# The softmax rows of a two-layer decoder trunk are scaled on Pool, head by head, instead of on VectorE and ScalarE

## The chip, the core and the metric

The kernel runs on one core of a Trainium2 chip. The metric is device microseconds (us) of one execution. The kernel before takes 322.24 us, the median of 3 runs (322.04 to 323.86). Five engines work side by side, each through its own queue in a fixed order: TensorE (PE, with its weight loads as PEld), VectorE (DVE), ScalarE (ACT), GpSimd (POOL, "Pool" in the text) and SyncE (SP), which here issues the loads of the weights. They meet at semaphores.

## The reference, cut to what matters

Two layers; x is 256 tokens by 1024 features, float32. In each layer

```
mod = silu(c) @ W_ada + b_ada -> (shift, scale, gate)
h   = RMSNorm(x) * (1 + scale) + shift
[q_A k_A v_A g_A | q_B k_B v_B g_B] = h @ W_in          (1024 x 4096)
A: 8 heads of 64, mixture of three causal dilated window attentions
B: 8 heads of 64, block-sparse attention (256 tokens are one block, so plain causal)
y   = RMSNorm([o_A*silu(g_A) | o_B*silu(g_B)] @ W_out);  x <- x + gate * y
```

q and k carry a partial rotary turn. For both branches the kernel computes softmax(scores + mask) @ v for each head: with 256 tokens the mixture of branch A is one softmax whose mask holds the logarithm of how many of the three patterns see a key. The change concerns one step of that softmax: the division of each row of exponentials by its sum.

## The kernel before, in words

Weights arrive by DMA as "pieces" of 128 x 1024 float32 (tile raw, 6 buffers). To keep float32 accuracy on PE, each is split in two: ACT copies the leading bits to whi (L205), DVE subtracts whi from raw and gets wlo (L212, 128 x 512 each). PE then makes three products for each k-tile, hi x whi, lo x whi and hi x wlo (L513; L526 for the gate chunks). A raw buffer comes free, and SP issues the next load, once DVE has made wlo of it. Other pieces are rows of W_ada; DVE "folds" those into running sums (L364, tiles acc_g and acc_ss).

PE's order is written out by hand as a list of slots (one slot is half a chunk of the input projection for 128 tokens), and the attention of two heads (a "pair") is threaded between slots: st_T (transposes of q and k), st_S one slot later (scores), st_X two slots after st_S (transposes of the softmax rows, L625), st_V one or two slots later (times v). There are 16 pairs: 4 of branch A and 4 of B in each layer. The text numbers them 1 to 16 in the order of the program; 1 to 8 are layer 0. The other engines' orders are made by a scheduler from the program; each engine then works through its queue strictly in that order.

The softmax step in st_S, for the two heads i of a pair, in tile z (128 x 384: queries 0-127 with keys 0-127, and queries 128-255 with all 256 keys):

- L601, DVE: scores plus mask into z, with the row minimum; L604, ACT: exponential, with the row sum into den.
- L608, DVE: one reciprocal of the four sums of the pair, rc.
- L614 and L612: the four blocks of z times rc. Three go to DVE (128, 256 and 128 columns), and one, the second head's 256 columns, to ACT (the table NACT picks it).

Then PE transposes z (L625). qkl (L579) is a DVE subtraction for the next pair's scores that reads the PSUM tile "t"; L625 needs a buffer of that tile, so it can wait for L579 too.

Pool has little to do: constants and two small inputs at the start, zeroing acc_g once a layer (L352), and the one-column arithmetic of the norms (L462 to L465).

Of the kernel before, what the change touches and what calls it, by code (L numbers as in the profile page):

```python
# [9 lines left out]
F32 = mybir.dt.float32  # L10
F32R = mybir.dt.float32r
I32 = mybir.dt.int32
AF = mybir.ActivationFunctionType
# [3 lines left out]
P = 128  # L17
# [5 lines left out]
# Slots: one product of half a chunk each, counted in a layer up to 32. Pairs of values: one for each layer.  # L23
# Where the heads of a branch start, and the distance of scores, transposes and outputs from there
AT_A, AT_B = ((12, 10), (22, 22))
# where branch A is gated; where the gate and the second token tile's h are made
# [4 lines left out]
# buffers for weights as loaded and for their two parts  # L31
NRAW, NHI, NLO = (6, 9, 8)
FOLD = 2048
# how far the splitting of weights runs ahead; what goes to the scalar engine; where W_ada's parts are due
AHEAD = (-12, 4)
H_AT = (2, 2)
NACT = (3,)
XACT = (0, 1)
ADA0, ADA1, ADA2 = ((2, 1), (6, 1), (23, 2))
# The start. GROUPS: k-tiles whose modulation is made together. FIRST_LOADS: a, b W_ada of a group, f a k-tile of  # L40
# W_in for the first two chunks, s, v quarters of chunks 2 and 5. FIRST_STEPS: T small inputs, R rotary tables, K masks,
# n, x norm and transposes of x, a, b, m modulation of a group, h, l its h in two parts, f, g a weight piece in two
# parts, p its products, w, y and s, v the same for chunks 2 and 5, k products that keep the array busy.
# [7 lines left out]
# theta ** (-2 i / RD) in float32  # L51
# [5 lines left out]
def turn_constants():  # L57
    """For units 2^20, 2^8, 2^-4: frac(unit / 2 pi) cut into parts of 12 bits, over the unit."""
    from fractions import Fraction
    pi = Fraction("3.14159265358979323846264338327950288419716939937510582097494459230781640628620899")  # L60
    rows = []
    for e in (20, 8, -4):
        u = Fraction(2) ** e
        f = u / (2 * pi)
        f -= f.numerator // f.denominator
        f1 = Fraction((f * 4096).numerator // (f * 4096).denominator, 4096)
        g = f - f1
        f2 = Fraction((g * 2 ** 24).numerator // (g * 2 ** 24).denominator, 2 ** 24)
        f3 = g - f2
        rows.append([float(f1 / u), float(f2 / u), float(f3 / u)])  # L70
    return rows
# [3 lines left out]
def trunk(ctx: ExitStack, tc: tile.TileContext, x, c, positions, pre_gain, post_gain,  # L75
# [19 lines left out]
    # ---------------------------------------------------------------- small inputs  # L95
    # rows: positions, c, the gains of the first norm, the shift and scale parts of b_ada
# [15 lines left out]
    # ---------------------------------------------------------------- weight stream  # L112
# [6 lines left out]
    def load_weights(src, key, r0, c0):  # L119
        """Two k-tiles of 512 columns"""  # L120
        nc.sync.dma_start(piece(key), src[r0:r0 + 2 * P, c0:c0 + CW].rearrange("(k p) n -> p k n", p=P))

    def load_first(key):
        """A k-tile for the first two chunks"""
# [3 lines left out]
    def load_group(key):  # L128
        """W_ada's columns for the shift and scale of a group of features: some of the rows"""
# [8 lines left out]
    def load_ada(key):  # L138
        """i < KT: a k-tile, the shift or the scale of all features; else the gate, a k-tile"""
# [25 lines left out]
    # Order of the weight stream: with each layer's products, what the next modulation needs.  # L165
    # a, b: W_ada for a group of features; f: the rows of W_in that it scales; s, v: quarters of other chunks
# [10 lines left out]
    # what the modulation needs, after the halves named  # L177
# [20 lines left out]
    def split_piece(key, a, b, low=True):  # L198
        """Parts a to b of a piece: hi holds the first 12 bits of each weight, lo the other 12."""
# [19 lines left out]
    # ---------------------------------------------------------------- constants  # L219
# [7 lines left out]
    # the table set of Silu serves until the first Exp  # L227
# [4 lines left out]
    # masks, to be added to minus the scores: [queries 0-127 x keys 0-127 | queries 128-255 x keys 0-255]  # L232
# [31 lines left out]
    # silu(c) and the gains of the first norm by feature on partitions  # L264
# [19 lines left out]
    def make_rope():  # L284
        # rotary tables: the angle in turns, reduced exactly, for any position
# [48 lines left out]
    # ---------------------------------------------------------------- modulation  # L334
# [31 lines left out]
    def mod_of(l, part, nb=4):  # L366
        """Rows 0, 32, .. of part in columns: [feature in its block, block, row]."""
# [11 lines left out]
    def ada_sum(l):  # L379
        """Sums over partitions of acc; 512 features to each group of 32 columns of the array."""  # L380
# [67 lines left out]
    def gate_end(l, h):  # L448
        """Sums over partitions of acc, on every partition, times the gain of the second norm."""
# [7 lines left out]
    # ---------------------------------------------------------------- norms  # L457
    def rstd_of(ms, other=None):
        """(sum of means + EPS) ** -0.5"""
# [10 lines left out]
    def parts_of(l, g):  # L470
        """hi and lo of half the features of h (or of a branch's output), for all tokens"""
# [32 lines left out]
    # ---------------------------------------------------------------- products with weights  # L504
    def product(bank, act, t, key, first, last, part=None):
        """The four k-tiles of a half, or two of them."""
# [9 lines left out]
    def gate_product(bank, act, u, key, hf):  # L516
        """Features 256 u to 256 (u + 1) of a chunk on partitions, all tokens: the weights stay, h streams."""
# [12 lines left out]
    # ---------------------------------------------------------------- attention  # L530
# [36 lines left out]
    def st_T(br, p):  # L567
# [5 lines left out]
        # the first 128 queries and keys; for the others, queries and all keys in two parts  # L573
# [10 lines left out]
    def st_S(br, p):  # L584
# [11 lines left out]
        den = ap.tile([P, 2, NT, 2], F32, name="den", bufs=4)  # L596
        pp = []
        for i in range(2):
            z = ap.tile([P, NS], F32, name="z", bufs=4)
            for t, (a, b) in enumerate(SC):  # L600
                nc.vector.tensor_tensor_reduce(z[:, a:b], bank[i][:, a:b], masks[br][:, a:b], 1.0, 3.0e38,  # L601
                                               ALU.add, ALU.min, accum_out=den[:, 0, t, i:i + 1])
            for t, (a, b) in enumerate(SC):
                nc.scalar.activation(z[:, a:b], z[:, a:b], AF.Exp, bias=den[:, 0, t, i:i + 1], scale=-1.0,  # L604
                                     accum_out=den[:, 1, t, i:i + 1])
            pp.append(z)
        rc = ap.tile([P, NT, 2], F32, name="rc", bufs=2)
        nc.vector.reciprocal(rc, den[:, 1])  # L608
        for i in range(2):
            for t, (a, b) in enumerate(SC):  # L610
                if 2 * t + i in NACT:
                    nc.scalar.activation(pp[i][:, a:b], pp[i][:, a:b], AF.Copy, scale=rc[:, t, i:i + 1])  # L612
                else:
                    nc.vector.tensor_scalar_mul(pp[i][:, a:b], pp[i][:, a:b], rc[:, t, i:i + 1])  # L614
# [19 lines left out]
    def st_V(br, p):  # L634
        """Outputs of two heads: [feature, token]"""
# [19 lines left out]
    def finish(br, p, src=None):  # L655
        """Outputs of two heads times the gate, in two parts"""
# [38 lines left out]
    # ---------------------------------------------------------------- the program  # L695
# [46 lines left out]
    def first_product(q, j, ci):  # L742
        """k-tile 2 q + j with chunk ci, both token tiles"""
# [14 lines left out]
    def early(t, part):  # L758
        """The first half of chunk 5, kept in the memory until the second one is due."""
# [33 lines left out]
    def keep_clock(n):  # L793
        """Products that nothing reads: the array's clock stays down until it has been busy for a while."""
# [134 lines left out]
```

## Time and profile before

| what | value |
|---|---|
| median of 3 runs | 322.24 us (322.04 to 323.86) |
| span of the profiled execution, the only time the profile gives of it | 321.5 us |
| PE, DVE, ACT, Pool busy | 299.6, 245.6, 203.5, 12.3 us |
| Pool instructions | 46 |
| mean granted TensorE clock | 0.996 of full speed |

The span is 0.7 us under the median of the runs. An engine's busy time counts the rows of its instructions; rows of neighbours overlap by a little on PE, DVE and ACT, so that three DVE products of 0.28, 0.35 and 0.28 us show as one merged entry of 0.74 us. In an answer on waits, the engine named first sat idle and the one behind the arrow ended it.

### The profile page before, as it was taken

Reading aid. Unit: us, or ns where it says so; the run is one execution under the profiler, and the core shown is the slowest. Engines: PE = TensorE matmul, PEld = TensorE weight load, DVE = VectorE, ACT = ScalarE, POOL = GpSimd, SP = SyncE. Lnnn points to the kernel's source line nnn. Section 1 sums busy time; section 2 is a strip of 40 time slices with the busy share of each in tenths; the row PEclk is TensorE's granted clock in tenths of the full one; section 3 lists DMA queues with packets and bytes.
Section 4 is the critical chain, followed back from the end, with each engine's and each line's share of the span. In section 5 each row is a group of like instructions: output and inputs, shape, how many; then the busy total and the mean of one; then the engine's idle time right before and its main releaser. Section 6 shows DMA issues by size and latency. Waiting matters only on the chain.

```text
span 321.5 us, 5293 instructions
## 1 busy us (share of the span) xinstructions
PE 299.6 (93%) x1817; PEld 237.6 (74%) x1817; DVE 245.6 (76%) x637; ACT 203.5 (63%) x435; POOL 12.3 (4%) x46
## 2 busy tenths in 40 slices
PE   0898899989999999999999899999999999999992
PEld 0565475867777789877687688877777799997881
DVE  4866773998998989898879899789785566786122
ACT  3646161959777469879568457578675579984100
POOL 3100001000000000000020300000000000000001
PEclk9999999999999999999999999999999999999998
DMA  8999988899798787586858549997765433000011
GB/s 253 342 351 302 346 262 308 293 348 317 247 302 265 259 287 202 173 280 233 285 185 282 178 129 303 350 320 231 228 215 177 132 132 131 2 1 2 0 65 65
DMA packets 37394, 70.63 MB, mean 220 GB/s; under 512 B 2492, under 2 KB 12790, under 8 KB 37368
## 3 DMA queue, kind: packets, MB, share of 16 engines
q1 hardware_dynamic: 36960, 69.22, 65.7%
q10 hardware_dynamic: 408, 1.09, 0.9%
q8 instruction: 14, 0.23, 0.3%
q14 instruction: 12, 0.10, 0.1%
HBM read 69.24 MB, written 1.05 MB: 219 GB/s over the span
## 4 chain that ended last, share of the span: by engine, by line
PE 57%; DMA 14%; DVE 13%; ACT 10%; issue 2%; SPq 1%; POOL 1%; ACTq 0%; DVEq 0%; POOLq 0%
PE mm L513 31%; PE mm L526 7%; DMA raw<-in_w_in_dram 5%; DVE wlo L212 4%; DMA raw<-in_w_ada_dram 4%; ACT whi L205 4%; DMA raw<-in_w_out_dram 3%; PE mm L753 3%; ACT z L604 3%; PE o L642 3%; PE o L414 2%; PE t L625 2%; DVE acc_ss L364 2%; DMA rows<-in_b_ada_dram 1%; PE t L513 1%
## 5 line engine op out<-in xcount | busy, mean ns | idle before, releaser
L212 DVE TENSOR_TENSOR wlo<-raw,whi 128x512 fp32r<-128x512 f32 x160 | 102.4, 685 | 8.0 <-PE mm L513 3.1
L205 ACT ACTIVATE whi<-raw 128x1024 fp32r<-128x1024 f32 (+1 forms) x88 | 84.4, 979 | 37.2 <-DMA raw<-in_w_in_dram 19.8
L513 PE MATMUL mm<-whi,hi 128*128 128x512 f32 x200 | 81.7, 408 | 0.0
L513 PE MATMUL mm<-wlo,hi 128*128 128x512 f32 x200 | 79.1, 395 | 0.0
L513 PE MATMUL mm<-whi,lo 128*128 128x512 f32 x200 | 79.0, 395 | 0.0
L513 PEld LDWEIGHTS mm<-whi,hi 128*128 128x128 f32 x200 | 37.6, 188 | 10.5 <-issue 1.7
L513 PEld LDWEIGHTS mm<-wlo,hi 128*128 128x128 f32 x200 | 37.6, 188 | 8.8
L513 PEld LDWEIGHTS mm<-whi,lo 128*128 128x128 f32 x200 | 37.7, 189 | 8.1 <-DVE lo L502 0.5
L526 PE MATMUL mm<-hi,whi 128*128 128x256 f32 x128 | 37.2, 291 | 0.0
L526 PE MATMUL mm<-hi,wlo 128*128 128x256 f32 x128 | 36.1, 282 | 0.0
L526 PE MATMUL mm<-lo,whi 128*128 128x256 f32 x128 | 36.0, 281 | 0.0
L604 ACT ACTIVATE z<-z,den 128x128 f32<-128x128 f32 x64 | 28.3, 445 | 3.8 <-DVE den L601 3.8
L526 PEld LDWEIGHTS mm<-hi,whi 128*128 128x128 f32 x128 | 24.1, 188 | 1.2 <-issue 0.2
L526 PEld LDWEIGHTS mm<-lo,whi 128*128 128x128 f32 x128 | 24.2, 189 | 0.2
L526 PEld LDWEIGHTS mm<-hi,wlo 128*128 128x128 f32 x128 | 24.1, 188 | 0.0
L364 DVE SCALAR_TENSOR_TENSOR acc_g<-raw,cs,acc_g 128x1024 f32<-128x1024 f32 x16 | 20.5, 1281 | 4.1 <-DMA raw<-in_w_ada_dram 4.1
L687 DVE TENSOR_TENSOR tmp<-mm,gate 128x512 f32<-128x512 f32 x8 | 5.5, 688 | 16.8 <-ACT sq L685 16.8
L364 DVE SCALAR_TENSOR_TENSOR acc_ss<-raw,cs,acc_ss 128x1024 f32<-128x1024 f32 x14 | 17.5, 1276 | 0.0
L685 ACT ACTIVATE sq<-mm 128x512 f32<-128x512 f32 x8 | 4.7, 593 | 19.8 <-PE mm L513 19.8
L625 PE MATMUL t<-ident,z 128*128 128x128 f32 x96 | 15.0, 282 | 2.4 <-DVE qkl L579 1.1
L625 PEld LDWEIGHTS t<-ident,z 128*128 128x128 f32 x96 | 10.6, 140 | 6.2 <-issue 1.7
L628 ACT ACTIVATE pT<-t 128x384 f32<-128x384 f32 x32 | 14.0, 491 | 1.2 <-PE t L625 1.2
(173 smaller groups left out, 454.9 us busy)
## 6 DMA issues: line engine op xcount, KB each, us to landing
raw<-in_w_in_dram SPq DMA_DIRECT2D x64, 512.0 KB, 5.2
raw<-in_w_ada_dram SPq DMA_DIRECT2D x32, 512.0 KB, 4.7
raw<-in_w_ada_dram SPq DMA_DIRECT2D x32, 256.0 KB, 5.0
raw<-in_w_out_dram SPq DMA_DIRECT2D x16, 512.0 KB, 5.1
xs<-in_x_dram SPq DMA_DIRECT2D x2, 512.0 KB, 4.3
gate<-in_post_norm_gain_dram ACTq DMA_DIRECT2D x2, 512.0 KB, 4.9
out_dram<-xs SPq DMA_DIRECT2D x4, 256.0 KB, 2.1
rows<-in_b_ada_dram ACTq DMA_DIRECT2D x2, 8.0 KB, 4.9
```

The costliest lines, as they stand in the source:

```text
L205: nc.scalar.activation(hi_q[key][:, a:b, :], raw[:, a:b, :], AF.Copy)
L212: nc.vector.tensor_sub(lo[:, d, :], raw[:, d, :], hi[:, d, :].bitcast(F32))
L364: nc.vector.scalar_tensor_tensor(a[:, sl], r[:, sl], cs[:, k:k + 1], a[:, sl], op0=ALU.mult, op1=ALU.add)
L414: nc.tensor.matmul(pm[32 * j:32 * j + 32, :w], csz[:, k, :], r[:, i * w:(i + 1) * w], start=k < 4, stop=k >= 4, tile_position=(0, 32 * j))
L513: nc.tensor.matmul(bank, a[:, k, t, :], w[:, k % 2, :], start=first and k + i == 0, stop=last and k == KH - 1 and i == 2)
L526: nc.tensor.matmul(bank[:, b * S:(b + 1) * S], w[:, k % 2, c0:c0 + P], a[:, k].rearrange("p t q -> p (t q)"), start=hf + b + k + i == 0, s ...
L604: nc.scalar.activation(z[:, a:b], z[:, a:b], AF.Exp, bias=den[:, 0, t, i:i + 1], scale=-1.0, accum_out=den[:, 1, t, i:i + 1])
L625: nc.tensor.transpose(pt[:, b * P:(b + 1) * P], pp[i][:, b * P:(b + 1) * P], ident)
L628: nc.scalar.activation(d, pt[:, :NS], AF.Copy)
L642: nc.tensor.matmul(ob[i * HD:(i + 1) * HD, q0:q0 + P], v[:, t, h], res[i][:, c0:c0 + P], start=t == 0, stop=n != 1, tile_position=(0, i * HD))
L687: nc.vector.tensor_mul(yg[:, sl], yb.pop((t, cc)), gate[l][:, sl])
L753: nc.tensor.matmul(mm[0, ci, t], a[:, k, t, :], w[:, ci, :], start=q == 0 and j == 0 and i == 0, stop=q == 3 and j == 1 and i == 2)
```

## The change

The reciprocal is taken for each head (of two sums, not four) as soon as that head's exponentials are there, and all four blocks of z are multiplied on Pool, two after each reciprocal. The products on DVE (L614) and on ACT (L612) and the table NACT are gone. The comments are also taken out, so that line numbers in the changed kernel are 1 to 3 lower (L608 is the reciprocal in both; the product on Pool is L610, wlo is L211, the fold L363, qkl L578).

```
-NACT = (3,)
...
-        den = ap.tile([P, 2, NT, 2], F32, name="den", bufs=4)
+        dens = ap.tile([P, 2, 2, NT], F32, name="den", bufs=4)
+        rcs = ap.tile([P, 2, NT], F32, name="rc", bufs=2)
         pp = []
         for i in range(2):
+            den, rc = dens[:, i], rcs[:, i]
             z = ap.tile([P, NS], F32, name="z", bufs=4)
...
-                                               ALU.add, ALU.min, accum_out=den[:, 0, t, i:i + 1])
+                                               ALU.add, ALU.min, accum_out=den[:, 0, t:t + 1])
...
-                nc.scalar.activation(z[:, a:b], z[:, a:b], AF.Exp, bias=den[:, 0, t, i:i + 1], scale=-1.0,
-                                     accum_out=den[:, 1, t, i:i + 1])
+                nc.scalar.activation(z[:, a:b], z[:, a:b], AF.Exp, bias=den[:, 0, t:t + 1], scale=-1.0,
+                                     accum_out=den[:, 1, t:t + 1])
+            nc.vector.reciprocal(rc, den[:, 1])
+            for t, (a, b) in enumerate(SC):
+                nc.gpsimd.tensor_scalar_mul(z[:, a:b], z[:, a:b], rc[:, t:t + 1])
             pp.append(z)
-        rc = ap.tile([P, NT, 2], F32, name="rc", bufs=2)
-        nc.vector.reciprocal(rc, den[:, 1])
-        for i in range(2):
-            for t, (a, b) in enumerate(SC):
-                if 2 * t + i in NACT:
-                    nc.scalar.activation(pp[i][:, a:b], pp[i][:, a:b], AF.Copy, scale=rc[:, t, i:i + 1])
-                else:
-                    nc.vector.tensor_scalar_mul(pp[i][:, a:b], pp[i][:, a:b], rc[:, t, i:i + 1])
         pr[br, p] = pp
```

The orders of PE and SP are the same in both kernels. What the scheduler makes of DVE's queue shows at two places. The first is pair 7 (layer 0, branch B, third pair), DVE from the last subtraction before the reciprocal on. Before:

```order
L364 SCALAR_TENSOR_TENSOR acc_ss<-raw,cs,acc_ss 128x1024 x2
L608 RECIPROCAL rc<-den 128x4
L212 TENSOR_TENSOR wlo<-raw,whi 128x512
L614 TENSOR_SCALAR z<-z,rc 128x128
L614 TENSOR_SCALAR z<-z,rc 128x256
L614 TENSOR_SCALAR z<-z,rc 128x128
L579 TENSOR_TENSOR qkl<-t,qkh 128x384
```

and with the change:

```order
L211 TENSOR_TENSOR wlo<-raw,whi 128x512 x3
L608 RECIPROCAL rc<-den 128x2
L363 SCALAR_TENSOR_TENSOR acc_ss<-raw,cs,acc_ss 128x1024
L608 RECIPROCAL rc<-den 128x2
L578 TENSOR_TENSOR qkl<-t,qkh 128x384
L363 SCALAR_TENSOR_TENSOR acc_ss<-raw,cs,acc_ss 128x1024
L211 TENSOR_TENSOR wlo<-raw,whi 128x512 x3
```

A fold now stands between the two heads' reciprocals. The same stands in pairs 1, 3 and 8; in pairs 2, 4, 5 and 6 it is one wlo subtraction.

The second place is layer 1, DVE in pair 10 (branch A, second pair), with the change:

```order
L363 SCALAR_TENSOR_TENSOR acc_g<-raw,cs,acc_g 128x1024
L608 RECIPROCAL rc<-den 128x2 x2
L546 TENSOR_TENSOR ra<-qk,cose 128x128
L547 TENSOR_TENSOR rb<-qk,sine 128x8x8
L548 TENSOR_TENSOR rb<-qk,sine 128x8x8
L549 TENSOR_TENSOR qk<-ra,rb 128x8x16
L578 TENSOR_TENSOR qkl<-t,qkh 128x384
L211 TENSOR_TENSOR wlo<-raw,whi 128x512 x4
```

Here, and in five more of the eight pairs of layer 1, both reciprocals stand together, behind whatever DVE did before, with nothing between the heads.

On Pool the products stand in the order of the pairs, with the zeroing of acc_g for layer 1 between two of them:

```order
L610 TENSOR_SCALAR z<-z,rc 128x128
L610 TENSOR_SCALAR z<-z,rc 128x256
L351 MEMSET acc_g 128x1024
L610 TENSOR_SCALAR z<-z,rc 128x128
```

That zeroing waits for DVE's subtraction of the layer's gate; in the changed order the products of pair 4 stand behind it.

## Rows read from the trace of the kernel before

**Rows 1.** Page, part 1: engine, busy us (share of the span) xinstructions.
```profile
PE 299.6 (93%) x1817; PEld 237.6 (74%) x1817; DVE 245.6 (76%) x637; ACT 203.5 (63%) x435; POOL 12.3 (4%) x46
```

**Rows 2.** Page, part 4: chain of waits that ended last, shares by engine.
```profile
PE 57%; DMA 14%; DVE 13%; ACT 10%; issue 2%; SPq 1%; POOL 1%; ACTq 0%; DVEq 0%; POOLq 0%
```

**Rows 3.** Waits of PE: who ended its idle time, us in total, times, longest.
```profile
PE t L625 <- DVE qkl L579: 1.1, 4, 0.4
...
PE t L625 <- DVE z L614: 0.8, 2, 0.5
PE t L625 <- ACT z L612: 0.4, 1, 0.4
```

**Rows 4.** Groups by line and shape, DVE: xcount | busy us, mean ns | idle before.
```profile
L212 DVE TENSOR_TENSOR wlo<-raw,whi 128x512 fp32r<-128x512 f32 x160 | 102.4, 685 | 8.0 <-PE mm L513 3.1 <-ACT whi L205 2.3 <-PE mm L526 2.2
L364 DVE SCALAR_TENSOR_TENSOR acc_g<-raw,cs,acc_g 128x1024 f32<-128x1024 f32 x16 | 20.5, 1281 | 4.1 <-DMA raw<-in_w_ada_dram 4.1
...
L614 DVE TENSOR_SCALAR z<-z,rc 128x128 f32<-128x128 f32 x32 | 9.0, 282 | 0.2
...
L614 DVE TENSOR_SCALAR z<-z,rc 128x256 f32<-128x256 f32 x16 | 5.6, 348 | 0.0
...
L608 DVE RECIPROCAL rc<-den 128x4 f32<-128x4 f32 x16 | 2.8, 176 | 8.5 <-ACT z L604 8.5
```

**Rows 5.** Groups by line and shape, ACT.
```profile
L612 ACT ACTIVATE z<-z,rc 128x256 f32<-128x256 f32 x16 | 8.1, 505 | 3.6 <-DVE rc L608 3.6
```

**Rows 6.** Timeline, pair 7: start us, length us, engine line op.
```profile
136.50 0.18 ACT L604 ACTIVATION_READ_ACCUMULATOR z<-z,den 128x1 f32 x1
...
137.38 0.19 ACT L604 ACTIVATION_READ_ACCUMULATOR z<-z,den 128x1 f32 x1
...
138.27 0.74 DVE L614 TENSOR_SCALAR z<-z,rc 128x128 f32<-128x128 f32 x3
...
138.70 0.61 PE L625 MATMUL t<-ident,z 128*128 128x128 f32 x3 [0.51 <-DVE z L614]
```

**Rows 7.** Timeline, pairs 11 and 14 (layer 1): DVE's products and PE's transposes.
```profile
233.53 0.75 DVE L614 TENSOR_SCALAR z<-z,rc 128x128 f32<-128x128 f32 x3
...
235.70 0.87 PE L625 MATMUL t<-ident,z 128*128 128x128 f32 x6
...
268.64 0.75 DVE L614 TENSOR_SCALAR z<-z,rc 128x128 f32<-128x128 f32 x3
...
272.99 0.87 PE L625 MATMUL t<-ident,z 128*128 128x128 f32 x6
```

**Rows 8.** Timeline of Pool, with one read-out on ACT that Pool waited for.
```profile
1.24 0.20 POOL L223 MEMSET ones<- 128x128 f32 x1
...
95.70 0.95 POOL L352 MEMSET acc_g<- 128x1024 f32 x1 [39.71 <-DVE wlo L445]
163.73 0.30 POOL L464 TENSOR_SCALAR rstd<-ms 128x1 f32<-128x1 f32 x1 [67.08 <-ACT sq L685]
...
167.82 0.89 POOL L464 TENSOR_SCALAR rstd<-ms 128x1 f32<-128x1 f32 x1 [3.13 <-ACT tmp L481]
...
177.80 0.19 ACT L685 ACTIVATION_READ_ACCUMULATOR sq<-mm 128x1 f32 x1
...
178.09 0.30 POOL L464 TENSOR_SCALAR rstd<-ms 128x1 f32<-128x1 f32 x1 [8.72 <-ACT sq L685]
...
181.95 1.11 POOL L464 TENSOR_SCALAR rstd<-ms 128x1 f32<-128x1 f32 x1 [2.92 <-ACT tmp L481]
```

**Rows 9.** Timeline of DVE around two of those Pool rows: four subtractions each.
```profile
166.05 2.50 DVE L212 TENSOR_TENSOR wlo<-raw,whi 128x512 fp32r<-128x512 f32 x4
...
180.40 2.49 DVE L212 TENSOR_TENSOR wlo<-raw,whi 128x512 fp32r<-128x512 f32 x4
```

**Rows 10.** Busy time in a stretch of layer 0: us and (xcount) by engine.
```profile
130.00:140.00 10.00, 9.27 (x82) 8.12 (x80) 8.69 (x24) 8.34 (x20) 0.00 (x0) 1.00 0.65 197
```

**Rows 11.** Instructions that touch wlo, up to 140 us: PE, PEld, DVE.
```profile
0.00:140.00 140.00, 52.24 (x146) 27.48 (x146) 43.27 (x67) 1.00 0.88 285
```

## The prediction

> **What bounds the kernel now.** I read the page first. PE is busy 299.6 us of a 321.5 us span [rows 1], and the chain of waits that ended last runs through PE for 57%, through DMA for 14% and through DVE and ACT for 13% and 10% [rows 2]. So PE's own work sets the time almost everywhere, and the other engines matter where PE waits for them. Next, who makes PE wait. At the transposes of the softmax rows (L625) PE waited 0.8 us for DVE's products, 0.4 us for ACT's and 1.1 us for qkl, which stands in DVE's queue close to the products [rows 3]: 2.3 us. **That is nearly all this change can give back**: the start of the program, before the first pair, and the last products of PE are the same in both kernels, and PE's order is unchanged.
>
> Then the stages. In a stretch of layer 0 (130 to 140 us) PE is busy 9.27 of 10 us, DVE 8.69, ACT 8.34 and Pool not at all [rows 10]: three engines near their limit, one free. Up to 140 us DVE had made 67 pieces of wlo and PE had used them in 146 products [rows 11]. Two of either belong to the gate; the first 48 pieces are used twice (96 products), those of the gate chunks four times (48 products, 12 pieces), so 60 are used up and DVE is 5 ahead. No wait of PE for wlo is among the rows, so splitting is late nowhere, but its lead in layer 0 is small.
>
> Last, single pairs. In pair 7 the row sum of the last exponential is read out at 137.38 + 0.19 = 137.57; DVE's three products end at 138.27 + 0.74 = 139.01; PE began its transposes at 138.70 after a wait of 0.51 [rows 6]. I call the time from the last read-out to the last product the tail: 1.44 us. This pair is **bare**: its tail is on PE's path. Read in the same way, pairs 1, 4, 5, 7, 8 and 9 are bare. The others have slack: in pair 11 the products end at 233.53 + 0.75 = 234.28 and PE comes at 235.70, 1.4 us later; in pair 14 the slack is 272.99 - 269.39 = 3.6 us [rows 7].
>
> **The change, part by part.**
>
> *Off DVE.* 32 products of 282 ns and 16 of 348 ns, 9.0 + 5.6 = 14.6 us, go; 16 reciprocals of 176 ns more come, 2.8 us (narrower ones, taken at the old price) [rows 4]. Net 11.8 us less of 245.6. Most of it shortens work that PE does not wait for.
>
> *Off ACT.* 16 products of 505 ns, 8.1 us [rows 5]. ACT's exponentials stand in one queue with its weight conversions, so in layer 0 they can come a little earlier.
>
> *Onto Pool.* 64 products. The trace has no wide product on Pool. The nearest rows are a one-column product with a scalar from memory, 0.30 us when undisturbed, and zeroings of 128 and 1024 columns, 0.20 and 0.95 us [rows 8], whose slope is 0.75 / 896 = 0.84 ns a column. My estimate is 0.30 + 128 x 0.00084 = 0.41 us and, for 256 columns, 0.51 us: 0.92 us a head. Lower end: 0.30 each, 0.60 a head, if columns cost nothing. Upper end: twice the slope, since a zeroing writes and reads nothing, 0.51 and 0.73, 1.24 a head. I take the middle; it is nearest to rows that have many columns. All 64: 29.4 us, on an engine busy 12.3 [rows 1]. The hand-over to Pool takes 0.10 us: a sum was read out at 177.80 + 0.19 = 177.99 and Pool began at 178.09 [rows 8]. The Trainium skill, "GPSIMD Engine Reference" (section 3.1), gives 769 ns for 512 elements and about 1.8 cycles an element at best, so by its figures the two products are some 0.49 and 0.68 us, inside my ends; no row here shows it.
>
> *The tail in a bare pair, nothing in the way.* Reciprocal 0.18, hand-over 0.10, two products 0.92, the first head being done: 1.20 us against 1.44, so 0.24 less. In pairs 4, 5 and 9 the order puts only one wlo (685 ns), or nothing, between the reciprocals, and the heads' exponentials end 0.88 us apart [rows 6], so the first head is out of the way: 3 x -0.24 = -0.7.
>
> *What stands in the way.* Pool has six one-column products with a scalar from memory. Two took 0.89 and 1.11 us in place of 0.30 [rows 8], and just those two began while DVE was at four subtractions in a row, each of two inputs from SBUF [rows 9]. They ended at 168.71 and 183.06; the subtractions at 168.55 and 182.89. So a Pool product waits for such a DVE instruction. Wlo and the folds are of this kind: 102.4 us and, in acc_g alone, 20.5 us [rows 4]. This is the price to weigh. The Trainium skill, "SBUF — State Buffer" (Who interferes with whom), says that a DVE instruction with two SBUF inputs and a GpSimd instruction that reads SBUF share a port pair, locked for a whole instruction, the later one blocked. That a Pool row is stretched agrees (1.11 us for 0.30). By that rule Pool waits for one DVE instruction and DVE for one Pool product; the rows leave open whether Pool gets in between two subtractions, since at 182.89 a whole run was over.
>
> I charge one DVE instruction. In pairs 1, 7 and 8, all bare, the order has a fold of 1.28 us [rows 4] right behind the first reciprocal. It begins about 0.9 us before the last read-out and ends 0.4 after it; then both heads' products follow, 0.92 + 0.92. The tail is about 2.25 us: 0.8 more, 3 x 0.8 = +2.4. The pairs with slack hide the same delay, except pair 11: the fold behind its reciprocals would end at about 233.5 + 1.3 = 234.8 and the four products at 236.6, while PE turns to the second head at 235.70 + 0.87 / 2 = 236.1 [rows 7]; of these 0.5 us I take +0.2, since Pool may get in first. DVE in turn waits for Pool. Bound: nothing, if they never meet, or all 29.4 us; with both at work about two thirds of the time, up to 20. Against the 11.8 us saved, DVE ends between 12 us better and 8 worse, most of it in the shadow of PE (the lead of 5 pieces). I take zero for it.
>
> *Relief.* Of the 2.3 us of waits, I credit 0.9 for earlier exponentials and an earlier qkl, since the three products no longer stand before it. Sum: -0.7 + 2.4 + 0.2 - 0.9 = **+1.0 us**. The profiled span becomes 322.5; with the 0.7 us by which the median stands above the span, **323.2 us**.
>
> **The rivals.**
>
> 1. *Pool is locked out for runs* (slower). If Pool gets in only when DVE idles or reads PSUM, a product waits for the whole run: four subtractions are 2.49 us [rows 9]. Places where the changed order has such a run behind the second reciprocal: pair 7 (fold and three wlo behind qkl), pair 8 (two wlo), pair 4 (rotary products and wlo, all of two inputs), pair 11 (fold, then four wlo). It decides from the point where the run exceeds the tail's 0.24 us of gain, or the slack. Price: about 2.5, 1.5, 1.5 and 1.0, 6.5 us in all, of which layer 0 has nothing to hide it: 322.2 + 6.5 = 328.7. For it: in [rows 8, 9] both Pool rows ended only 0.16 us after the whole run. Against it: the later part of those runs may simply have been the one instruction Pool met. Chance 0.25.
>
> 2. *The locks rarely meet* (faster). Pool finds gaps while DVE waits for ACT at the reciprocals; then every bare pair gains and the waits vanish: 322.2 - 2.3 = 319.9. For it: DVE sat idle 8.5 us before the reciprocals [rows 4], just when Pool would start. Against it: the second reciprocal now comes behind a fold in three bare pairs. Chance 0.13.
>
> 3. *Head by head is in name only.* In six pairs of layer 1 both reciprocals stand together, so the first head does not start earlier, and in layer 1 all but pair 9 have slack: 322.2, no change. Chance 0.07.
>
> **How the numbers follow.** My forecast, 321 to 325, has 0.55. A run of this kernel can tell about 1% (3.2 us) from no change. Faster by more than that needs 319.0 or less, below rival 2's own figure; I give it 0.04, out of rival 2. Slower by more than that, above 325.5, is rival 1 and a little of the forecast's upper end (products at 1.24 us a head add 0.64 to the tail of each bare pair that a fold delays, 1.9 us over three): 0.29. The rest is 0.67. The range goes from 320.3, near rival 2, to 327.5, into rival 1's lower half, and leaves some 0.08 below and 0.1 above.
>
> **What would show it.** The Pool rows of L610: 0.41 and 0.51 us when DVE is idle or at PSUM, longer by up to 1.28 us beside wlo and folds. Rows beyond 2 us would mean runs (rival 1). DVE's wlo and fold means should rise above 685 and 1281 ns if Pool locks DVE out. PE's waits at L625 should name Pool, most in pairs 1, 7 and 8, and stay away in 10 and 12 to 16. If they are gone, rival 2 holds. What would make the forecast wrong is a Pool product of well over 1 us without any DVE neighbour, or DVE losing so much to Pool that weight loads come late in layer 0, which would show as PE waits at L512 on wlo.

## The result and the profile after

The changed kernel takes **340.09 us** (median of 4 runs, 338.47 to 342.46), the kernel before, run beside it, 322.44 us (322.04 to 323.86): a ratio of 1.0538, 95% interval 1.0487 to 1.0589. The prediction said 323.2 us, at most 327.5. The profiled execution took 338.86 us, its span is 337.1 us against 321.5 before.

First the page of the changed kernel: busy time by engine, and the shares of the chain of waits. They answer to [rows 1] and [rows 2].

```profile
PE 305.2 (91%) x1817; PEld 241.7 (72%) x1817; DVE 240.9 (71%) x605; ACT 199.6 (59%) x419; POOL 80.0 (24%) x110
...
PE 52%; DVE 12%; DMA 12%; POOL 10%; ACT 6%; issue 5%; ACTq 1%; DVEq 0%; POOLq 0%; SPq 0%
```

DVE lost only 4.7 us of work and ACT 3.9 (the prediction had 11.8 and 8.1), Pool gained 67.7, and Pool, 1% of the chain before, now has a tenth of it. PE does the same 1817 instructions and is busy 5.6 us longer; that is a second loss, below. Now the waits of PE, which answer to [rows 3]:

```profile
PE t L622 <- POOL z L610: 9.7, 10, 1.5
...
PE t L622 <- DVE qkl L578: 2.4, 1, 2.4
```

Three kinds of wait of 2.3 us became two of 12.1. The span's 15.6 us are nearly accounted for: 9.7 of waits for Pool less the 1.2 for the old products, 2.4 for qkl less 1.1, and 5.6 of longer PE work, together 15.4. Why Pool is late shows in its own groups by shape:

```profile
L610 POOL TENSOR_SCALAR z<-z,rc 128x256 f32<-128x256 f32 x32 | 38.1, 1192 | 0.0
L610 POOL TENSOR_SCALAR z<-z,rc 128x128 f32<-128x128 f32 x32 | 30.6, 955 | 145.7 <-DVE rc L608 134.8 <-PE o L451 7.5 <-PE mm L512 3.4
```

in the least, median and longest duration (ns) of its 64 products, from the view of that line:

```profile
L610 POOL TENSOR_SCALAR z<-z,rc x64: 601/926/3342, 75.5 to 304.8; 128x128 f32<-128x128 f32 x32, 128x256 f32<-128x256 f32 x32
```

and in its timeline, of which these are pairs 1, 8, 13 and 14:

```profile
75.47 5.56 POOL L610 TENSOR_SCALAR z<-z,rc 128x128 f32<-128x128 f32 x4 [20.20 <-DVE rc L608]
...
153.41 6.86 POOL L610 TENSOR_SCALAR z<-z,rc 128x128 f32<-128x128 f32 x4 [4.66 <-DVE rc L608]
...
275.89 2.99 POOL L610 TENSOR_SCALAR z<-z,rc 128x128 f32<-128x128 f32 x4 [18.07 <-DVE rc L608]
283.43 2.99 POOL L610 TENSOR_SCALAR z<-z,rc 128x128 f32<-128x128 f32 x4 [4.55 <-DVE rc L608]
```

The last two rows are the plain length: 2.99 us for a pair's four products, where the prediction had 1.84. The trace shows what decides between plain and long: of the 32 products of 256 columns, the 17 that began while DVE was at no instruction with two inputs from SBUF took 0.92 to 0.94 us, the other 15 took 1.00 to 1.96. In pair 1 the same four took 5.56 us and in pair 8 6.86. Had every pair taken 2.99, Pool would have needed 16 x 2.99 = 47.8 us; it took 67.7, so 19.9 us are stretching. What stood beside the longest product (pair 8, the first one) shows in the timelines of Pool and DVE:

```profile
153.41 3.34 POOL L610 TENSOR_SCALAR z<-z,rc 128x128 f32<-128x128 f32 x1 [4.66 <-DVE rc L608]
...
153.16 1.26 DVE L363 SCALAR_TENSOR_TENSOR acc_ss<-raw,cs,acc_ss 128x1024 f32<-128x1024 f32 x1
154.35 0.16 DVE L608 RECIPROCAL rc<-den 128x2 f32<-128x2 f32 x1
154.42 1.27 DVE L211 TENSOR_TENSOR wlo<-raw,whi 128x512 fp32r<-128x512 f32 x2
155.61 0.75 DVE L657 TENSOR_TENSOR oo<-oo,gs 128x256 f32<-128x256 f32 x2
156.49 0.69 DVE L211 TENSOR_TENSOR wlo<-raw,whi 128x512 fp32r<-128x512 f32 x1
```

A product that needs 0.60 us when nothing is in the way ended at 156.75, after a fold, two subtractions and the two products oo, all with two inputs from SBUF and all but back to back. And DVE hardly paid for that; these groups answer to [rows 4], the last line being the fold of acc_ss in the kernel before:

```profile
L211 DVE TENSOR_TENSOR wlo<-raw,whi 128x512 fp32r<-128x512 f32 x160 | 104.6, 695 | 8.4 <-PE mm L512 4.0 <-ACT whi L204 3.1 <-PE mm L525 0.8
...
L363 DVE SCALAR_TENSOR_TENSOR acc_ss<-raw,cs,acc_ss 128x1024 f32<-128x1024 f32 x14 | 18.3, 1311 | 0.0
...
L364 DVE SCALAR_TENSOR_TENSOR acc_ss<-raw,cs,acc_ss 128x1024 f32<-128x1024 f32 x14 | 17.5, 1276 | 0.0
```

A subtraction is 10 ns longer than before, some 1.6 us over 160 of them. Last, the granted clock, in the column behind Pool's busy time, in stretches of the kernel before (first fence) and of the changed one (second):

```profile
70.00:220.00 150.00, 146.66 (x897) 118.41 (x895) 135.19 (x325) 107.81 (x226) 5.81 (x9) 1.00 0.78 256
```

```profile
81.50:84.90 3.40, 3.40 (x16) 2.79 (x16) 2.02 (x9) 3.12 (x10) 0.00 (x0) 0.50 0.75 290
139.50:142.90 3.40, 3.40 (x17) 3.40 (x17) 3.40 (x13) 3.37 (x7) 0.00 (x0) 0.51 0.34 124
160.00:163.40 3.40, 3.07 (x9) 2.49 (x10) 0.94 (x2) 2.29 (x4) 0.28 (x1) 0.50 0.51 169
```

Before, PE had its full 2.4 GHz in this stretch. Now it falls to the 1.2 GHz level three times, each time when PE had stood at the transposes: for Pool in pairs 1 and 8, for qkl in pair 6. PE's last wait before or at each fall:

```profile
81.08 0.44 PE L622 MATMUL t<-ident,z 128*128 128x128 f32 x2 [1.30 <-POOL z L610]
...
138.21 0.52 PE L622 MATMUL t<-ident,z 128*128 128x128 f32 x3 [2.43 <-DVE qkl L578]
...
160.33 0.69 PE L622 MATMUL t<-ident,z 128*128 128x128 f32 x2 [0.58 <-POOL z L610]
```

Pair 1 had two shorter waits (0.76 and 0.81 us) ahead of that row, pair 8 two longer ones (1.14 and 0.71), and the third fall, at 160.0, lies within the last wait. Three stretches of 3.4 us at half speed would do the work of 5.1 us, an estimate that is nearly all of PE's extra 5.6.

### The profile page after: what moved, and what is told of

Same layout as the page of the kernel before. It is cut to its first block, busy times and chain, and to the rows that moved or that the text cites. A ratio compares the mean times of both kernels' runs of the same rounds, so it can differ in the third digit from the quotient of the medians.

```text
span 337.1 us, 5409 instructions
## 1 busy us (share of the span) xinstructions
PE 305.2 (91%) x1817; PEld 241.7 (72%) x1817; DVE 240.9 (71%) x605; ACT 199.6 (59%) x419; POOL 80.0 (24%) x110
## 3 DMA queue, kind: packets, MB, share of 16 engines
HBM read 69.24 MB, written 1.05 MB: 209 GB/s over the span
## 4 chain that ended last, share of the span: by engine, by line
PE 52%; DVE 12%; DMA 12%; POOL 10%; ACT 6%; issue 5%; ACTq 1%; DVEq 0%; POOLq 0%; SPq 0%
PE mm L512 26%; POOL z L610 9%; PE mm L525 8%; DMA raw<-in_w_in_dram 7%; DVE wlo L211 4%; DMA raw<-in_w_ada_dram 3%; PE mm L750 3%; ACT whi L204 3%; PE o L639 2%; PE o L413 2%; PE t L622 2%; DMA rows<-in_b_ada_dram 2%; PE t L512 1%; DVE z L603 1%; PE s L591 1%
## 5 line engine op out<-in xcount | busy, mean ns | idle before, releaser
L211 DVE TENSOR_TENSOR wlo<-raw,whi 128x512 fp32r<-128x512 f32 x160 | 104.6, 695 | 8.4 <-PE mm L512 4.0
L610 POOL TENSOR_SCALAR z<-z,rc 128x128 f32<-128x128 f32 x64 | 67.7, 1074 | 145.7 <-DVE rc L608 134.8
L512 PE MATMUL mm<-whi,hi 128*128 128x512 f32 x200 | 82.8, 414 | 0.0
L512 PE MATMUL mm<-whi,lo 128*128 128x512 f32 x200 | 79.8, 399 | 0.0
L525 PE MATMUL mm<-hi,whi 128*128 128x256 f32 x128 | 38.0, 297 | 0.0
L525 PE MATMUL mm<-lo,whi 128*128 128x256 f32 x128 | 36.7, 287 | 0.0
L622 PE MATMUL t<-ident,z 128*128 128x128 f32 x96 | 16.6, 287 | 12.4 <-POOL z L610 9.7
L525 PEld LDWEIGHTS mm<-hi,whi 128*128 128x128 f32 x128 | 24.8, 194 | 1.2 <-issue 0.2
L525 PEld LDWEIGHTS mm<-lo,whi 128*128 128x128 f32 x128 | 25.0, 195 | 0.2
L363 DVE SCALAR_TENSOR_TENSOR acc_g<-raw,cs,acc_g 128x1024 f32<-128x1024 f32 x16 | 20.5, 1283 | 2.5 <-DMA raw<-in_w_ada_dram 2.5
L363 DVE SCALAR_TENSOR_TENSOR acc_ss<-raw,cs,acc_ss 128x1024 f32<-128x1024 f32 x14 | 18.3, 1311 | 0.0
```

Source lines behind the costliest of these rows:

```text
L211: nc.vector.tensor_sub(lo[:, d, :], raw[:, d, :], hi[:, d, :].bitcast(F32))
L363: nc.vector.scalar_tensor_tensor(a[:, sl], r[:, sl], cs[:, k:k + 1], a[:, sl], op0=ALU.mult, op1=ALU.add)
L512: nc.tensor.matmul(bank, a[:, k, t, :], w[:, k % 2, :], start=first and k + i == 0, stop=last and k == KH - 1 and i == 2)
L525: nc.tensor.matmul(bank[:, b * S:(b + 1) * S], w[:, k % 2, c0:c0 + P], a[:, k].rearrange("p t q -> p (t q)"), start=hf + b + k + i == 0, s ...
L610: nc.gpsimd.tensor_scalar_mul(z[:, a:b], z[:, a:b], rc[:, t:t + 1])
L622: nc.tensor.transpose(pt[:, b * P:(b + 1) * P], pp[i][:, b * P:(b + 1) * P], ident)
```

## The experiments

All ratios are to the kernel before, run on the same chip; the chips differ between groups of experiments, so times of different groups are compared by their ratios. "Theory" in the first four expectations is that Pool's products are the cause and head-by-head order is not.

**1. Head by head, without Pool.** Only the products go back, three to DVE and one to ACT.

```
-                nc.gpsimd.tensor_scalar_mul(z[:, a:b], z[:, a:b], rc[:, t:t + 1])
+                if 2 * t + i == 3: nc.scalar.activation(z[:, a:b], z[:, a:b], AF.Copy, scale=rc[:, t:t + 1])
+                else: nc.vector.tensor_scalar_mul(z[:, a:b], z[:, a:b], rc[:, t:t + 1])
```

> The changed kernel with its reciprocals head by head, but the four products of a pair back on DVE (three) and ACT (one). Theory (the price of a product on Pool makes the tails long, head by head is harmless): 322 us, 320 to 324, no Pool rows, PE waits at the transposes of about 2 us as before. Rival (the new order of DVE, with folds between the reciprocals, makes the tails long): 330 us or more.

Measured: 324.6 us, ratio 1.0054 (1.0016 to 1.0092). That is 0.6 us above the theory's range and far from the rival's 330: the sixteen more reciprocals and the new order cost half a per cent, of 5.4.

**2. Pool, without head by head.** The kernel before with its one reciprocal a pair, and all four products on Pool.

```
-                if 2 * t + i in NACT: ... nc.scalar.activation ... else: ... nc.vector.tensor_scalar_mul
+                nc.gpsimd.tensor_scalar_mul(pp[i][:, a:b], pp[i][:, a:b], rc[:, t, i:i + 1])
```

> The kernel before with its one reciprocal for a pair, but all four products on Pool. Theory (price on Pool): a pair needs 2 x (0.605 + 0.925) = 3.06 us on Pool after the last row sum, where the changed kernel has half of that done by then; so slower than the changed kernel: 343 us, 338 to 349. Rival (head by head is what costs): 322 to 326.

Measured: 348.02 us, ratio 1.0765 (1.0709 to 1.0822). PE waits longer and more often for Pool:

```profile
PE t L622 <- POOL z L611: 17.4, 18, 1.6
```

So Pool is the cause, and starting after the first head is worth some 7 us (2.3% by the ratios) once Pool does the work.

**3 and 4. One slot more for the softmax,** in the changed kernel and, as its control, in the one before: the transposes of z and the products with v come one slot later.

```
-    OS, OX, OV = ((1, 1), (3, 3), (4, 5))
+    OS, OX, OV = ((1, 1), (4, 4), (5, 6))
...   (and out_product(l, 0, 1, 0) is moved up behind slot 32)
```

> The changed kernel with PE's transposes of z and all that follows one slot later (2.8 us or more of other products in between). Theory (only the late z costs, through PE's waits): the slot covers most of Pool's 4.3 us for a pair, PE's waits for Pool fall from 9.7 us to under 2, the clock stays up: 323 us, 320 to 327. Rival (DVE loses time to Pool at the shared port and weights come late): 333 us or more, with PE waiting for wlo.

> The control: the kernel before with the same shift of one slot. Both theories: its 2.3 us of waits at the transposes go, 320 us, 319 to 322.5.

Measured: 336.67 us, ratio 1.0406 (1.0342 to 1.0469), and 331.4 us, ratio 1.0249 (1.0195 to 1.0304). Both expectations missed, because the shift costs by itself. The waits of PE, of the changed kernel shifted and then of the one before shifted, say why (the profiled execution of the first kernel took 340.5 us, its other three runs 335.3 to 337.3, so its row is read for the kind of wait alone):

```profile
PE t L570 <- ACT pT L625: 11.5, 8, 5.0
```

```profile
PE t L571 <- ACT pT L628: 7.7, 8, 2.0
```

The next pair's transposes of q and k now stand right behind those of z, and the two buffers of the PSUM tile t come free only when ACT has copied the rows out. What the pair of runs still says: against its own control Pool costs some 5 us, not 17.6, and waits for Pool's z no longer appear. The first time lies in its rival's range, but what the rival named, PE waiting for wlo, is not among the waits. Slack is a cure, but here it can't be had for nothing.

**5. Pool writes, but doesn't read.** Memsets in place of the products.

```
-                nc.gpsimd.tensor_scalar_mul(z[:, a:b], z[:, a:b], rc[:, t:t + 1])
+                for r in range(4 + 2 * t):
+                    c = a + P * (r % (1 + t))
+                    nc.gpsimd.memset(z[:, c:c + P], 0.005)
```

> The changed kernel with each Pool product replaced by zeroes that Pool writes into the same rows, 4 or 6 memsets of 128 columns, chosen to last about as long as an undisturbed product (0.605 and 0.925 us); Pool reads nothing, and this kernel leaves out the scaling by the reciprocal. Theory (Pool's reading meets VectorE's two-operand instructions, which makes 49 us of undisturbed products into 68.7): Pool takes about 3.1 us in every pair, none 5 to 7, the waits of PE for Pool's z fall from 9.7 us to under 5, and the time is 327 to 334 us. Rival (a Pool pass of any kind is stretched the same way, or the bare length is the price): 337 to 341 us.

Measured: 325.02 us, ratio 1.0062 (1.0025 to 1.0099), faster than either theory allowed. But these writes need no reciprocal, and Pool began them as soon as ACT's exponentials were done, before DVE's reciprocal. So the run left two explanations open.

**6. Keep PE busy while it waits.** 41 products that nothing reads (the expectation has 38, a slip in adding) ahead of the transposes where PE waited.

```
+                if (len(done), i, b) in FILL:
+                    keep_clock(FILL[len(done), i, b])
                 nc.tensor.transpose(pt[:, b * P:(b + 1) * P], pp[i][:, b * P:(b + 1) * P], ident)
```

> The changed kernel with 38 products that nothing reads put on PE at the eight places where it waited longest for Pool's z, so that PE stays busy while it waits. Theory (the stalls of pairs 1, 6 and 8 pull the granted clock to 0.5 for three stretches of 3.4 us, and that is some 5 of the 16 us): the granted clock stays at 1.0 up to 170 us, and the time is 333 to 337 us although PE has more to do. Rival (the clock's fall lies in time that is lost anyway): 339 to 342 us.

Measured: 341.2 us, ratio 1.0559 (1.0508 to 1.061): the theory's time missed, and the rival's came. But PE is busy 311.1 us, 5.9 more, and still waits 8.7 us for Pool; Pool's delays moved to other pairs, and the clock fell once, at 153 us. So the run as a whole does not decide between the two. One place is clean, the work from the end of pair 1's transposes to the start of pair 2's, in the changed kernel and then with fillers:

```profile
81.50:90.82 9.32, 9.32 (x51) 7.34 (x51) 6.48 (x21) 5.06 (x14) 3.43 (x4) 0.82 0.54 186
```

```profile
82.18:89.95 7.77, 7.77 (x50) 6.09 (x51) 7.14 (x22) 4.40 (x15) 4.56 (x4) 1.00 0.96 362
```

The same work, 50 instructions, takes 7.77 us at a granted clock of 1.00 and 9.32 at 0.82: one fall costs 1.55 us. That three of them cost three times that in the total is worked out, not shown.

**7 and 8. Pool in the pairs with slack alone, and in the others alone.** Pairs 10 and 12 to 16 had shown no wait.

```
+                if len(made) in SLACK:        (SLACK = 9, 11 .. 15; the other kernel has "not in")
                     nc.gpsimd.tensor_scalar_mul(z[:, a:b], z[:, a:b], rc[:, t:t + 1])
+                elif ...                      (ACT and DVE as in experiment 1)
```

> Head by head as in the changed kernel, but Pool has the products of pairs 10 and 12 to 16 alone, where PE showed no wait for them; the other ten pairs have them on VectorE and ScalarE. Theory (a Pool product costs only where nothing else is queued for PE behind it): the same as with all products on VectorE and ScalarE head by head, 323 to 326 us. Rival (Pool's products also slow VectorE's splitting of weights everywhere): 327 to 331 us.

> The complement of the kernel with Pool's products in six pairs alone: Pool has all four products of the other ten pairs (1 to 9 and 11), VectorE and ScalarE those of pairs 10 and 12 to 16, head by head. Theory (the whole price is paid in these ten pairs): 336 to 341 us, the changed kernel's time. Rival (every Pool product costs something wherever it stands): 330 to 335 us.

Measured: 325.28 us, ratio 1.0074 (1.0041 to 1.0108), and 338.25 us, ratio 1.0503 (1.0399 to 1.0607). With Pool in six pairs the time is that of experiment 1; with Pool in the other ten it is that of the change. Within what the intervals can tell, the price is paid where PE comes early, and nowhere else. Slack is not a fixed property of a pair, though: in the first of the two kernels Pool took 4.75 us in pair 10, and PE waited 1.3 us for it.

**9, 11 and 12. Fewer products on Pool, and which.** The first head's two; the second head's two (DVE has the first head's); the first head's 256 columns alone.

```
+                if i == 0:              (experiment 12: if i == 0 and t == 1)
                     nc.gpsimd.tensor_scalar_mul(...)
+                elif ...                (ACT and DVE as in experiment 1)
...
+                eng = nc.gpsimd if i else nc.vector          (experiment 11)
+                eng.tensor_scalar_mul(z[:, a:b], z[:, a:b], rc[:, t:t + 1])
```

> Head by head; in every pair Pool has the products of the first head alone, VectorE and ScalarE those of the second. Pool's work in a pair halves to 1.53 us undisturbed, beside VectorE's. Theory (the price is Pool's four products in series, 3.1 to 6.9 us a pair, after which PE can go on): the time falls to 325 to 331 us, with PE's waits for Pool under 4 us. Rival (the first blocks set it, which come no earlier): 335 to 340 us.

> Head by head; in every pair Pool has the two products of the second head alone, VectorE both of the first. Pool has as few products as with the first head alone (which cost nothing, 322.84 us), but they end last in the pair. Theory (what decides is when the pair's last product ends against PE's arrival): 327 to 335 us, PE waiting for Pool's z in pairs 1, 3, 8, 9 and 11. Rival (the length of Pool's queue of four decides): 322 to 326 us.

> Head by head; Pool has one product of a pair, that of the first head's 256 columns, and the others stay on VectorE and ScalarE. Theory (that product has the second head's exponentials and products to hide behind, and a fourth of VectorE's load in it goes): 321 to 324.5 us, no different from the kernel before within 1%; PE is busy 299 of 322 us, so that nothing more is to be won there. Rival (VectorE's relief shows once Pool ends nothing last): under 320 us.

Measured: 322.84 us, ratio 0.9988 (0.9959 to 1.0017); 327.8 us, ratio 1.0129 (1.005 to 1.0209); 321.21 us, ratio 0.9954 (0.9917 to 0.9991). The first is better than its theory had it (325 to 331); the second, whose runs went from 325.81 to 333.77 us, lies at the lower edge of its theory's range. With the first head alone Pool's products are stretched too. These are its groups (first fence) and PE's wait for them (second):

```profile
L614 POOL TENSOR_SCALAR z<-z,rc 128x256 f32<-128x256 f32 x16 | 17.2, 1074 | 0.0
L614 POOL TENSOR_SCALAR z<-z,rc 128x128 f32<-128x128 f32 x16 | 14.1, 884 | 162.2 <-DVE rc L611 140.2 <-PE o L452 13.0 <-PE o L451 9.0
```

```profile
PE t L631 <- POOL z L614: 1.0, 2, 0.7
```

31.3 us of Pool work in place of 23.9 (16 times half of 2.99), but the second head's exponentials and products on the other engines cover it, and PE waits 1.0 us. With the second head, as many products, nothing is left to cover them: PE waits 6.9 us, 5.0 of that at pair 4. (The expectation named pairs 1, 3, 8, 9 and 11; the waits came in 1, 4 and 6.) Pool's row of pair 4 and PE's longer wait there:

```profile
103.01 6.77 POOL L611 TENSOR_SCALAR z<-z,rc 128x128 f32<-128x128 f32 x2 [5.80 <-DVE rc L608]
...
108.21 0.48 PE L623 MATMUL t<-ident,z 128*128 128x128 f32 x1 [3.85 <-POOL z L611]
```

Two products that need 1.50 us took 6.77, the first of them 5.14 in place of 0.60, while DVE went from one two-input instruction to the next (rotary products, subtractions, two folds) from 102.74 to 108.98. Behind that wait the granted clock was 0.50 from 108.2 to 115.0 us, which is part of this kernel's price. So it is not the length of Pool's queue alone, but what Pool has last. Experiment 12 lets Pool have the one product with most cover; it is the fastest kernel of this study, 0.5% under the kernel before (too little to call it faster), with PE busy 299.3 us of a span of 320.0. Its rival (under 320 us) did not come: there is little more to win here.

**10 and 13. Writes that wait for the reciprocal.** Two tries at holding the memsets of experiment 5 back. In 10 Pool first overwrites rc.

```
+            nc.gpsimd.memset(rc, 1.0)
+            ...  3 and 6 memsets of 128 columns of z
```

> As the kernel with Pool's zeroes in place of its products, but Pool first overwrites the head's reciprocals, so that it starts when VectorE has made them, as in the changed kernel; then 3 and 6 memsets of 128 columns a head, some 3.1 us a pair. The scaling is left out. Theory (what the product's read pays at VectorE's two-operand instructions is most of the price, and 3.1 us a pair behind the reciprocals are nearly covered): 324 to 329 us, no wait of PE for Pool over 1 us. Rival (the kernel without that dependence was spared because Pool began before the reciprocal): 332 to 339 us.

Measured: 327.42 us, ratio 1.0129 (1.0045 to 1.0213). The scheduler put most memsets of z ahead of that of rc in Pool's queue (in pair 1 Pool began at 74.63, the reciprocal at 75.10), so this did not test what it was meant to. In 13 DVE writes the reciprocals into z itself, where the memsets must overwrite them:

```
-            nc.vector.reciprocal(rc, den[:, 1])
+            nc.vector.reciprocal(z[:, 0:2 * P].rearrange("p (t c) -> p t c", c=P)[:, :, 0], den[:, 1])
...
-                nc.gpsimd.tensor_scalar_mul(z[:, a:b], z[:, a:b], rc[:, t:t + 1])
+                for r in range(4 + 2 * t):
+                    nc.gpsimd.memset(z[:, a:a + P], 0.005)
```

> Pool's zeroes in place of its products once more, this time held back as the products are: VectorE writes a head's reciprocals into the first column of both blocks, which Pool's 4 and 6 memsets then overwrite, so that Pool can begin neither block before VectorE is done; some 3.2 us a pair, a little more than undisturbed products take. The scaling is left out. Theory (the stretching of Pool's products by VectorE's two-operand instructions is most of the price): 324 to 330 us, Pool 3.2 us in nearly every pair, waits of PE for Pool under 3 us in all. Rival (3.1 us behind the reciprocals is itself the price, the stretching only adds to it): 333 to 341 us, with waits of 5 us and more.

Measured: 327.53 us, ratio 1.0168 (1.0097 to 1.0239). Pool's timeline in pairs 1, 2, 4 and 8 (first fence), and the waits of PE (second):

```profile
74.43 3.45 POOL L610 MEMSET z<- 128x128 f32 x20 [20.36 <-DVE z L607]
81.71 3.46 POOL L610 MEMSET z<- 128x128 f32 x20 [3.83 <-DVE z L607]
...
100.15 3.45 POOL L610 MEMSET z<- 128x128 f32 x20 [4.00 <-DVE z L607]
...
147.07 3.51 POOL L610 MEMSET z<- 128x128 f32 x20 [5.83 <-DVE z L607]
```

```profile
PE t L622 <- DVE qkl L578: 3.0, 1, 3.0
PE t L622 <- POOL z L610: 2.3, 4, 0.8
```

Now Pool starts after DVE, works 0.46 us longer in a pair than undisturbed products do, and beside the same subtractions and folds it takes 3.45 to 3.51 us where the products took up to 6.86. The waits for Pool go from 9.7 to 2.3 us, and the price falls from 17.6 us over the kernel before to 5.3, by some 12 us. The rival, that the plain length is the price, is out. What is shown is that Pool's products are stretched beside DVE's two-input instructions and its zeroings are not. Length is not the reason: in the kernel before, a zeroing of 1024 columns took 0.95 us [rows 8] beside three subtractions in a row,

```profile
95.56 1.89 DVE L212 TENSOR_TENSOR wlo<-raw,whi 128x512 fp32r<-128x512 f32 x3
```

and one-column products were stretched from 0.30 to 1.11 us there. That it is the reading, and not the arithmetic, was not tried by itself. The Trainium skill, "SBUF — State Buffer" (Who interferes with whom), says just that: the contention is with Pool instructions that read SBUF, not with those that only write.

## Why the prediction was wrong, point by point

- **What bounds the kernel** was read rightly: PE, with the transposes of z as the place where the others reach it. "That is nearly all this change can give back" held too; no kernel here gained more than 0.5%.
- **One step that failed is the price, "Onto Pool".** The prediction took 0.41 and 0.51 us, at most 1.24 us a head. Undisturbed they are 0.60 us for 128 columns (the least in the row above) and 0.92 for 256 (seven of the sixteen in experiment 12, where it stands alone, took 0.92 to 0.94), 1.53 a head. A zeroing's slope [rows 8] says nothing of an instruction that reads, multiplies and writes: 2.5 ns a column against 0.84. With 1.53 in place of 0.92 the prediction's own sum would have been +1.1 in place of -0.7 for pairs 4, 5 and 9, +6.1 in place of +2.4 for pairs 1, 7 and 8, some +1.4 in place of +0.2 for pair 11, less the 0.9: +7.7 us, 330 us. By its own sum that alone is above the range, but what ran cost less: experiment 13, with a little more than the plain length on Pool, is 5.3 us over the kernel before, all told.
- **The step that cost most is "I charge one DVE instruction"**, in three pairs: the stretching came in all eight pairs of layer 0 and in four of layer 1 (9, 11, 15 and 16), and a single product could lose much more than the longest DVE instruction (3.34 us for 0.60). The prediction's own rows spoke against it: the one-column product that took 1.11 us in place of 0.30 [rows 8] lost 0.81 us, more than the 0.685 of one subtraction. By experiment 13 the stretching is some 12 of the 17.6 us, the clock's falls that it causes included. The other 5 hold the plain length, the head-by-head order and what pair 6 costs, for experiment 13 still has a wait of 3.0 us for qkl there and one fall of the clock behind it (133.8 us). The shares depend on each other: had Pool been faster there would have been cover for some of the stretching.
- **Rival 1 had the mechanism**, at 6.5 us. It named pair 8, pair 4 and pair 11 rightly and pair 7, where PE did not wait, wrongly, and the mark it set (rows beyond 2 us) was passed, but it was built on the short products and counted only the runs behind the second reciprocal. The rows don't support it in its pure form either: in most pairs Pool got in after one or two DVE instructions. Rival 2 is out. **Rival 3 is out**: experiments 1 and 2 show that head by head is real.
- **DVE would lose nothing to Pool, taken as zero:** right in its size; 10 ns on a subtraction, 35 on a fold of acc_ss. Of the two ends given (12 us better, 8 worse) neither shows: DVE's busy time fell by 4.7 us. One reason is that the 14.6 us counted for the products were rows that overlap; three of them occupy 0.74 us [rows 6], 11.8 in all 16 pairs. Weights came in time.
- **Which pairs:** none waited in 10 and 12 to 16, as said. Waits for Pool came in 1, 3, 4, 8, 9 and 11; pairs 5 and 7 had none, and 3 was not on the list.
- **The clock** was in no step. The stalls took it to its lower level three times, by estimate about 5 us, half as much as the waits for Pool. A sum that prices a stall by its own length is short.
- **The qkl wait** grew by 1.3 us in place of the relief of 0.9. It is 1.4, 0.7 and 0.2 us in experiments 1, 9 and 12, and 3.0 in 13 (4.7 in 5), where Pool reads nothing: Pool's reads don't bring it. The trace of pair 6 shows where it comes from. ACT stood 1.24 us for a piece of W_out to land, with a table load and the activation of the gate (L560) queued behind the conversion of that piece; DVE's products oo waited 1.27 us for the gate, and qkl stood in DVE's queue behind them and a fold (137.51). In the kernel before, ACT's wait for W_out came behind pair 6's copies:

```profile
128.19 0.49 ACT L577 ACTIVATE qkh<-t 128x384 fp32r<-128x384 f32 x1
...
131.12 1.06 ACT L205 ACTIVATE whi<-raw 128x1024 fp32r<-128x1024 f32 x1 [1.56 <-DMA raw<-in_w_out_dram]
```

So it is the scheduler's new order of ACT's queue; no run put the old order back, and that stays an argument from the trace.

## What to carry to other kernels

Before moving element-wise work to an idle Pool, take its price from a run of that very instruction at its shape, for no other row will do: the one wide Pool instruction before the change that reads its tile, a select of 128 columns, took 0.29 us against 0.60. And ask what DVE does in the same microseconds: beside back-to-back two-input DVE work a product took up to eight times its length here (5.14 us for 0.60), and DVE hardly felt it. Give Pool what has other engines' work behind it (here the first of two heads, at no cost) and never what the bottleneck waits for last. An off-path engine with a long, variable latency was worse here than a busy one with a short, steady one.

## What the runs showed that was not expected

- The asymmetry: over the whole kernel Pool's products lost 19.9 us to DVE, DVE's subtractions and folds some 2 us to Pool, no fold more than 0.22 at once. The Trainium skill, "SBUF — State Buffer" (SBUF: two separate sides), tells of a lock that goes to whoever issues first, for a whole instruction; by it Pool would have lost one DVE instruction at a time. The longest product here went on through several that were issued after it, so the measurement differs from that rule. It differs the other way round too: in pair 11 a fold began at 246.63, 0.13 us after a product that took its plain 0.61, and was not held up for the rest of it, for it took 1.31 us against 1.28.
- Writes are not stretched beside two-input work: 20 memsets of 128 columns took 3.45 us beside the same DVE work in nearly every pair. But they are beside a product of DVE with one tensor input, the 1024-column L361 that starts a running sum. The zeroing of acc_g for layer 1, 0.95 us in the other runs, began inside it in experiments 7 and 11 (rows below, in this order) and in experiment 1, where it took 1.50. In pair 3 of experiment 13, beside two such products, single memsets took 0.67 and 0.78 us in place of 0.21. And DVE feels Pool there: a 128-column product of 0.34 us (hf) that met the first zeroing took 1.06 before the change and 1.05 after. No experiment was made of it.

```profile
96.86 1.50 POOL L351 MEMSET acc_g<- 128x1024 f32 x1 [39.58 <-DVE wlo L444]
...
95.72 1.49 POOL L351 MEMSET acc_g<- 128x1024 f32 x1
```

- In the changed kernel a stall of 2.43 us for qkl, and three stalls of 0.6 to 1.3 us in one pair (twice), went with 3.4 us at half clock, 1.55 us of lost work in the one place that could be compared. Single stalls of 1.51, 1.32 and 1.19 us in pairs 3, 9 and 11 did not.
